# Moving the bias of three heads to GpSimd, holding exp(bias) in PSUM, and one store per batch, in a log-sum-exp kernel

## The chip, the cores and the metric

The kernel runs on one core of one Trainium2 chip. The metric is the device time of one execution in microseconds (us). The core has five engines, named in the profile as PE (TensorE), DVE (VectorE), ACT (ScalarE), POOL (GpSimd) and SP (SyncE, which issues the loads here). Sixteen DMA engines move data between HBM and SBUF.

## The reference

```python
def reference(x, bias):            # x [8, 2048, 2048] f32, bias [8, 256] f32
    B, S, D = x.shape
    H = bias.shape[0]
    Dh = D // H                    # 256
    x_heads = x.reshape(B, S, H, Dh).transpose(0, 2, 1, 3)
    x_heads = x_heads + bias[None, :, None, :]
    x_tiled = np.repeat(x_heads, 2, axis=2)
    mx = x_tiled.max(axis=-1, keepdims=True)
    lse = mx.squeeze(-1) + np.log(np.exp(x_tiled - mx).sum(axis=-1))
    return lse                     # [8, 8, 4096]
```

So for each row and each of eight heads the kernel needs log(sum(exp(x + bias))) over 256 elements, and stores each result twice. It reads 134 MB and writes 1 MB. The kernels leave out the maximum, which these inputs allow.

## The kernel before

The input is cut into 64 tiles of 256 rows (2 MB). In a tile each of 128 partitions holds K = 2 rows. Nine tile buffers take the loads, all issued by SP. The eight heads of a row go two ways:

- Heads 0 and 1 ("biased"): TensorE adds the bias by matmul into PSUM, ScalarE takes exp there and sums by its accumulator.
- Heads 2 to 7 ("weighed"): ScalarE takes exp(x) in place, and VectorE multiplies by exp(bias), which is held in SBUF, and sums, one instruction per head and row.

```python
    def weigh(v, h, dst):                       # L180: one head of one row
        nc.vector.tensor_tensor_reduce(out=j, in0=v, in1=w_rep[:, c : c + Dh],
            scale=1.0, scalar=0.0, op0=ALU.mult, op1=ALU.add, accum_out=dst)
    ...
    for t in range(T):
        for k0, k1, c0, c1 in pieces(t):        # one piece, except in the last two tiles
            ...
            if c0 == 0:
                got = add_bias([xt[:, k, 0:CPE] for k in range(k0, k1)])   # TensorE, L155, L160
            w0 = max(c0, CPE)
            if w0 < c1:
                exp_inplace(xt[:, k0:k1, w0:c1])                           # ScalarE, L174
            if c0 == 0:
                for k in range(k0, k1):
                    sum_biased(got[k - k0], lambda h: sum_at(k, h))        # ScalarE, L166
            for k in range(k0, k1):
                for c in range(w0, c1, Dh):
                    weigh(xt[:, k, c : c + Dh], c // Dh, sum_at(k, c // Dh))
        ...
        if t + NBUF < T:
            load(t + NBUF)
        ...                                     # every 8 tiles: transpose, Ln, store of a batch
```

A batch of 8 tiles ends in a 64-row result, 2 KB per row, which leaves in five stores of uneven row counts, such as `[16, 16, 16, 9, 7]` (the table `STORE_ROWS`).

The softmax here doesn't subtract the row's maximum and nothing guards it: scores larger than these inputs give would overflow.

## Time and profile before

| | before |
|---|---|
| time, median of 3 runs | 342.96 us (342.44 to 343.75) |
| span in the profile | 341.4 us |
| loads | about 429 GB/s while they run, 2 MB per 4.9 us |
| VectorE, one tile | 12 multiply-and-sums, 0.347 us start to start: 4.16 us |
| ScalarE, one tile | 4.44 us |
| matmuls of tile 61 start, having waited for its load | 321.5 us |
| from there to the end | 19.9 us |

First the page of the profile: the span, the busy line (busy us, share, number of instructions), the DMA share and the GB/s in 40 slices of the span, and two of the DMA queues (packets, MB, share of 16 engines' time). q1 carries the loads and stores; q14 fetches instructions.

```profile
span 341.4 us, 3425 instructions
...
PE 235.2 (69%) x410; PEld 69.7 (20%) x410; DVE 271.6 (80%) x1538; ACT 295.2 (86%) x597; POOL 10.4 (3%) x22
...
DMA  8999999999999999999999999999999999999910
GB/s 302 430 430 429 427 430 427 426 425 426 424 429 429 430 429 419 431 426 429 430 424 425 428 428 427 379 402 428 430 419 389 397 428 429 396 380 397 366 57 16
...
q1 hardware_dynamic: 11168, 135.17, 94.8%
...
q14 instruction: 20, 0.16, 0.1%
```

The DMA engines are busy from the first slice to the 38th. No compute engine is. So the stream of loads bounds the kernel, except for the last 20 us. The rate dips after slice 25. The loads share SP's queue with stores, which SP issues from 64 us on, so the stores alone do not say why the dips begin so late.

The groups of instructions (line, engine, operation, shapes, count, then busy us and mean ns of one, then idle time before them and what ended it):

```profile
L180 DVE CUSTOM_DVE_ANT_0 junk<-xt,w_rep 128x256 f32<-128x256 f32 x768 | 270.8, 422 | 65.7 <-ACT xt L174 65.6
...
L174 ACT ACTIVATE xt<-xt 128x3072 f32<-128x3072 f32 x62 | 171.2, 2762 | 24.5 <-DMA xt<-in_x_dram 19.9 <-DVE R L180 4.0
```

VectorE waits for ScalarE, and ScalarE waits for data. Both have time to spare per tile.

Stretches of 5 us (start and end; then busy us and number of instructions of PE, PEld, DVE, ACT, POOL; granted clock; DMA share; GB/s):

```profile
200.00:205.00 5.00, 4.15 (x10) 0.91 (x8) 4.24 (x24) 4.60 (x10) 0.00 (x0) 0.88 1.01 429
220.00:225.00 5.00, 4.60 (x12) 1.44 (x11) 4.35 (x26) 4.82 (x11) 0.00 (x0) 0.83 0.95 372
300.00:305.00 5.00, 4.43 (x8) 1.52 (x8) 4.36 (x27) 4.81 (x10) 0.00 (x0) 0.66 0.98 356
320.00:325.00 5.00, 4.10 (x6) 1.17 (x4) 4.27 (x25) 4.52 (x10) 0.00 (x0) 0.50 0.74 282
325.00:330.00 5.00, 5.00 (x10) 1.46 (x10) 5.00 (x31) 4.73 (x12) 0.00 (x0) 0.75 0.24 71
```

VectorE issues 24 to 27 counted instructions in 5 us, because each multiply-and-sum is followed by an instruction that reads the accumulator out. At 325 us the loads are over and VectorE is full.

Last, the timeline at tile 61 (start, duration, engine, instruction, and in brackets the idle time and what ended it), and the last Ln on ScalarE:

```profile
321.54 3.78 PE L160 MATMUL ps<-xt,ident 128*128 128x512 f32 x4 [0.90 <-DMA xt<-in_x_dram]
...
338.64 0.37 ACT L209 ACTIVATE res<-tps 8x256 f32<-8x256 f32 x1 [0.94 <-PE tps L196]
```

TensorE waits for tile 61 until 321.54 us.

### The profile page before, as it was taken

What the parts mean: (1) busy time and instruction counts of PE and PEld (TensorE: products, weight loads), DVE (VectorE), ACT (ScalarE), POOL (GpSimd) and SP (SyncE); (2) the same over time, 40 slices, a digit from 0 to 9 for tenths busy, and PEclk for the clock granted to TensorE, in tenths of its full rate; (3) what the DMA queues carried; (4) which work ended last, traced back from release to release, by engine and by line L of the source; (5) the groups of instructions that cost most, each with busy time, mean ns of one, the idle gap of its engine ahead of it and who ended that gap; (6) DMA issues with size and microseconds to landing.
All of it is one profiled execution on the core that took longest, in us unless ns stands there. A gap on an engine that the chain in (4) does not pass through costs nothing. (4 is left out here: it accounts for less than half of the span.)

```text
span 341.4 us, 3425 instructions
## 1 busy us (share of the span) xinstructions
PE 235.2 (69%) x410; PEld 69.7 (20%) x410; DVE 271.6 (80%) x1538; ACT 295.2 (86%) x597; POOL 10.4 (3%) x22
## 2 busy tenths in 40 slices
PE   6295788767786767775767775965775665775791
PEld 2121122112121112221121221321221221221220
DVE  0429999898887888887889688787798698797795
ACT  2389999998997998987997997998998998998895
POOL 6000000000000000000000000000000000000004
PEclk9999856885868885888885886588888888888585
DMA  8999999999999999999999999999999999999910
GB/s 302 430 430 429 427 430 427 426 425 426 424 429 429 430 429 419 431 426 429 430 424 425 428 428 427 379 402 428 430 419 389 397 428 429 396 380 397 366 57 16
DMA packets 11545, 135.50 MB, mean 397 GB/s; under 512 B 1913, under 2 KB 2185, under 8 KB 3329
## 3 DMA queue, kind: packets, MB, share of 16 engines
q1 hardware_dynamic: 11168, 135.17, 94.8%
q0 software_dynamic: 352, 0.10, 0.1%
q14 instruction: 20, 0.16, 0.1%
q8 instruction: 3, 0.05, 0.1%
q10 hardware_dynamic: 2, 0.01, 0.0%
HBM read 134.23 MB, written 1.05 MB: 396 GB/s over the span
## 5 line engine op out<-in xcount | busy, mean ns | idle before, releaser
L180 DVE CUSTOM_DVE_ANT_0 junk<-xt,w_rep 128x256 f32<-128x256 f32 x768 | 270.8, 422 | 65.7 <-ACT xt L174 65.6
L160 PE MATMUL ps<-xt,ident 128*128 128x512 f32 x256 | 184.3, 859 | 88.6 <-DMA xt<-in_x_dram 88.3
L174 ACT ACTIVATE xt<-xt 128x3072 f32<-128x3072 f32 (+3 forms) x70 | 177.7, 2541 | 24.5 <-DMA xt<-in_x_dram 19.9
L166 ACT ACTIVATE ps<-ps 128x256 f32<-128x256 f32 x256 | 94.6, 369 | 11.7 <-PE ps L160 6.7
L160 PEld LDWEIGHTS ps<-xt,ident 128*128 128x128 f32 x256 | 57.4, 248 | 173.2 <-DMA xt<-in_x_dram 124.2
L180 DVE DVE_READ_ACCUMULATOR2_ANT R<- 128x1 f32 x744 | 61.9, 83 | 0.0
L155 PE MATMUL ps<-b,ones 3*128 3x512 bf16 x128 | 46.6, 447 | 6.2 <-DVE R L180 6.2
L166 ACT ACTIVATION_READ_ACCUMULATOR ps<-ps 128x1 f32 x256 | 48.6, 190 | 0.0
L155 PEld LDWEIGHTS <-ones 3*128 3x128 bf16 x128 | 7.5, 97 | 74.5 <-issue 66.7
L230 POOL DMA_DIRECT2D out_dram<-res x8 | 4.0, 505 | 324.1 <-ACT res L209 324.1
L136 PE MATMUL ps<-brow,ones 1*128 1x512 f32 x6 | 5.5, 1074 | 3.2 <-DMA brow<-in_bias_dram 3.2
L209 ACT ACTIVATE res<-tps 64x512 f32<-64x512 f32 (+3 forms) x11 | 5.9, 540 | 1.4 <-PE tps L196 0.9
L143 ACT ACTIVATE w_rep<-ps 128x512 f32<-128x512 f32 x3 | 1.8, 597 | 5.5 <-PE ps L136 5.5
L196 PEld LDWEIGHTS tps<-ident,R 128*64 128x64 f32 (+1 forms) x16 | 2.7, 166 | 8.9 <-issue 4.7
L196 PE MATMUL tps<-ident,R 128*64 128x128 f32 (+1 forms) x16 | 4.3, 363 | 0.0
L196 PE MATMUL tps<-ident,Rz 128*8 128x128 f32 x2 | 0.7, 374 | 4.7 <-DVE Rz L180 4.7
L136 PEld LDWEIGHTS ps<-brow,ones 1*128 1x128 f32 x6 | 1.8, 321 | 5.3 <-issue 5.3
L110 ACT ACT_TABLE_LOAD x1 | 1.3, 1283 | 0.7 <-PEq L307 0.7
L132 POOL DMA_DIRECT2D b<-bparts x3 | 1.6, 553 | 0.0
L196 PEld LDWEIGHTS tps<-ident,Rz 128*8 128x8 f32 x2 | 0.2, 82 | 5.2 <-DVE Rz L180 2.6
L129 POOL TENSOR_TENSOR brest<-brest,bparts 1x512 f32<-1x512 f32 x1 | 1.1, 1146 | 0.1
L127 POOL TENSOR_TENSOR brest<-brow,bparts 1x512 f32<-1x512 f32 x1 | 1.1, 1144 | 0.1
(15 smaller groups left out, 5.7 us busy)
## 6 DMA issues: line engine op xcount, KB each, us to landing
xt<-in_x_dram SPq DMA_DIRECT2D x62, 2048.0 KB
xt<-in_x_dram SPq DMA_DIRECT2D x2, 1024.0 KB
xt<-in_x_dram SPq DMA_DIRECT2D x2, 512.0 KB
xt<-in_x_dram SPq DMA_DIRECT2D x3, 256.0 KB
out_dram<-res SPq DMA_DIRECT2D x17, 32.0 KB
xt<-in_x_dram SPq DMA_DIRECT2D x2, 128.0 KB
out_dram<-res POOLq DMA_DIRECT2D x8, 12.0 KB, 1.7
out_dram<-res SPq DMA_DIRECT2D x3, 24.0 KB
```

Of the source, the lines that this page charges most:

```text
L110: nc.scalar.add_instruction(mybir.InstLoadActFuncSet(name=nc.get_next_instruction_name(), act_func_set_id=set_idx,))
L132: nc.gpsimd.dma_start(out=b3[i : i + 1, :], in_=bparts[:, i])
L136: nc.tensor.matmul(ps[i], lhsT=ones, rhs=brow[:, CPE + c : CPE + c + MM], start=True, stop=True,)
L143: nc.scalar.activation(out=w_rep[:, c : c + MM], in_=ps[i], func=ACT.Exp)
L155: nc.tensor.matmul(p[:, 0:CPE], lhsT=ones3, rhs=b3, start=True, stop=False)
L160: nc.tensor.matmul(p[:, 0:CPE], lhsT=ident, rhs=v, start=False, stop=True)
L166: nc.scalar.activation(out=p[:, c : c + Dh], in_=p[:, c : c + Dh], func=ACT.Exp, accum_out=dst(h),)
L174: nc.scalar.activation(out=v, in_=v, func=ACT.Exp)
L180: nc.vector.tensor_tensor_reduce(out=j, in0=v, in1=w_rep[:, c : c + Dh], scale=1.0, scalar=0.0, op0=ALU.mult, op1=ALU.add, accum_out=dst,)
L196: nc.tensor.transpose(out=tps[i][0:nr, k], in_=src(k), identity=ident)
L209: nc.scalar.activation(out=rv, in_=tv, func=ACT.Ln)
L230: engine.dma_start(out=ov, in_=iv)
```

## The change

The intent is to relieve VectorE. In 62 of 64 tiles, three of the six weighed heads take another way: GpSimd adds their bias in SBUF ahead of exp (`g_add`), ScalarE takes exp one tile later, and VectorE sums all three heads of both rows with one instruction (`g_sum`). exp(bias) of the other heads lies in PSUM, so that VectorE's multiply reads only one operand from SBUF, while GpSimd works there. To make room, the PSUM buffers of the biased heads go from six to four, and the two of the transposes share one tile. A buffer is given back one tile later. And each batch leaves in one store of 64 rows, in place of five. The last two tiles stay on the old way.

```diff
 NPE = 2
+NG = 3
+NLATE = 2
 NBUF = 9
-STORE_ROWS = [
-    [15, 14, 13, 12, 10],
-    ...
-]
@@
-    w_rep = sb.tile([P, CW], F32, name="w_rep")
+    b_rep = sb.tile([P, NG * Dh], F32, name="b_rep")
@@
-    ps = [pp.tile([P, MM], F32, name=f"ps{i}") for i in range(6)]
+    w_rep = pp.tile([P, CW], F32, name="w_rep")
+    ps = [pp.tile([P, MM], F32, name=f"ps{i}") for i in range(4)]
... (the two transpose tiles become one; b_rep and w_rep are filled)
@@
+    def g_add(t):
+        nc.gpsimd.tensor_tensor(out=g_part(t), in0=g_part(t), in1=b_tile, op=ALU.add)
+
+    def g_sum(t):
+        b, blk = divmod(t, NBLK)
+        nc.vector.tensor_reduce(
+            out=R[b][:, :, NPE : NPE + NG, blk],
+            in_=g_part(t).rearrange("p k (h j) -> p k h j", j=Dh),
+            op=ALU.add,
+            axis=mybir.AxisListType.X,
+        )
@@
-            step, parts = n, STORE_ROWS[b]
+            step, parts = n, [nr]
@@
-        for k0, k1, c0, c1 in pieces(t):
+        if left >= NLATE:
+            got = add_bias([xt[:, k, 0:CPE] for k in range(K)])
+            g_add(t)
+            w0 = CPE + NG * Dh
+            exp_inplace(xt[:, :, w0:D])
+            if t:
+                exp_inplace(g_part(t - 1))
+            for k in range(K):
+                sum_biased(got[k], lambda h: sum_at(k, h))
+            for k in range(K):
+                for c in range(w0, D, Dh):
+                    weigh(xt[:, k, c : c + Dh], c // Dh, sum_at(k, c // Dh))
+            if t:
+                g_sum(t - 1)
+        for k0, k1, c0, c1 in pieces(t) if left < NLATE else []:
@@
-        if t + NBUF < T:
-            load(t + NBUF)
+        if left == NLATE:
+            exp_inplace(g_part(t))
+            g_sum(t)
+        if 0 < t and t - 1 + NBUF < T:
+            load(t - 1 + NBUF)
```

More of the change, by code (lines that the diff above doesn't have):

```diff
@@ L19 @@
 NPE = 2
+NG = 3
+NLATE = 2
 NBUF = 9
 LAST_CUTS = [[0, 1024, 2048], [0, 512, 1024, 1536, 1792, 2048]]
-STORE_ROWS = [
-    [15, 14, 13, 12, 10],
-    [11, 9, 16, 16, 12],
-    [16, 16, 16, 8, 8],
-    [16, 16, 16, 9, 7],
-    [16, 16, 16, 10, 6],
-    [16, 16, 16, 11, 5],
-    [16, 16, 16, 12, 4],
-]
 @with_exitstack
@@ L76 @@
     xts = [sb.tile([P, K, D], F32, name=f"xt{i}") for i in range(NBUF)]
-    ps = [pp.tile([P, MM], F32, name=f"ps{i}") for i in range(6)]
-    tps = [pp.tile([P, K, P], F32, name=f"tps{i}") for i in range(2)]
+    w_rep = pp.tile([P, CW], F32, name="w_rep")
+    ps = [pp.tile([P, MM], F32, name=f"ps{i}") for i in range(4)]
+    tpair = pp.tile([P, 2, K, P], F32, name="tpair")
+    tps = [tpair[:, i] for i in range(2)]
     def pieces(t):
@@ L132 @@
         nc.gpsimd.dma_start(out=b3[i : i + 1, :], in_=bparts[:, i])
-    for i, c in enumerate(range(0, CW, MM)):
+    for c in range(0, CW, MM):
         nc.tensor.matmul(
-            ps[i],
+            w_rep[:, c : c + MM],
             lhsT=ones,
@@ L142 @@
         )
-        nc.scalar.activation(out=w_rep[:, c : c + MM], in_=ps[i], func=ACT.Exp)
+    nc.scalar.activation(out=b_rep, in_=w_rep[:, 0 : NG * Dh], func=ACT.Copy)
+    for c in range(0, CW, MM):
+        w = w_rep[:, c : c + MM]
+        nc.scalar.activation(out=w, in_=w, func=ACT.Exp)
     n_ps = [0]
@@ L171, in sum_biased, with g_part @@
             )
+    b_tile = bass.AP(
+        tensor=b_rep.tensor,
+        offset=b_rep.offset,
+        ap=[b_rep.ap[0], [0, K], [1, NG * Dh]],
+    )
+    def g_part(t):
+        return xts[t % NBUF][:, :, CPE : CPE + NG * Dh]
+    def g_add(t):
[7 more added lines that the diff above has]
+            axis=mybir.AxisListType.X,
+        )
     def exp_inplace(v):
```

## The prediction

> **What bounds the kernel now.** The load stream. In the table of 5 us stretches the DMA share is about 1.0 from 5 to 320 us, at 420 to 433 GB/s for the first 210 us: a 2 MB tile every 4.9 us. In the timeline of a steady tile ScalarE needs 4.44 us (one 128x3072 exp, 2.65 us start to start, then four 128x256 exps with accumulator reads, 1.79 us) and VectorE 12 multiply-and-sums at 347 ns, 4.16 us. Both wait for data (groups: VectorE idle 65.7 us before the multiply-and-sum). The trace's landing times show one of 16 DMA engines drifting some 7 us behind the rest by the end; the instruction fetches in the span, 15 of 8 KB (0.32 us each) and three of 16 KB (1.06 us), would about explain it if all are on it (my inference). The tile-61 matmuls wait for data until 321.5 us. The tail after it, 17 us to the last Ln plus 2.7 us for the store, is compute: the chain of waits names ScalarE, and VectorE runs without a gap from 324.4 to 333.4 us.
>
> **What changes, per tile (62 of 64).**
> - GpSimd: one 128x1536 add. A 1x512 fp32 add took 1.146 us; scaled, 3.4 us, under 4.9. The multiply now has one input in PSUM, the sum has only one, so VectorE should not hold GpSimd off[...]. No run here shows it yet.
> - VectorE: six multiply-and-sums go, one 128x1536 sum comes[...], 1.7 us. 6x0.347+1.7 = 3.8 us.[...]
> - ScalarE: one 3072 exp becomes two of 1536 (1.37 us each in the tail): 4.53 us per tile. Still under 4.9; it catches up more slowly after the late start.
> - Buffers return one tile later; depth was 7 to 8 tiles, so no starvation.
> - Stores: one of 64 rows per batch instead of five uneven ones. It takes one place in the queue, so the dips to 360 to 400 GB/s after 210 us should shrink, but those are idle fast engines; the slowest decides.[...] fewer instruction fetches: -0.6 us.
>
> **Critical path.** Nothing saved on VectorE is on it in the stream. In the tail ScalarE has one more 1536 exp after tile 61 lands (tile 60's delayed group), +1.4 us; VectorE two sums for six multiplies, +1.3 us, overlapped. So 343 + 0.3 + 1.5 = 344.8 us.
>
> **Prediction: 344.8 us, 8 in 10 between 342.3 and 349. Faster by over 2%: 3%; within 2%: 86%; slower: 11%.**
>
> **Right or wrong by:** GpSimd adds at 3.2 to 3.6 us; sums at 1.7 us; multiply-and-sums every 0.35 to 0.41 us; ScalarE busy up about 5 us; tile 61 landing at 321 to 323 us; tail 21 to 22 us; DMA share still 1.0 until 320.
>
> **What would make it wrong:** GpSimd over 4.9 us per tile, or blocked by VectorE; PSUM reads much slower (VectorE near 4.9 us); the even stores delaying the slow DMA engine by several us; or the dips costing real time, so that the single store brings tile 61 up to 5 us earlier.

The sum: 343 + 0.3 + 1.5 = 344.8 us. The 0.3 in it is made of -0.6 us for the fetches and of +0.9 us for rows that the slow DMA engine would write more with even stores; without that term the sum would be 343.9 us. That VectorE should not hold GpSimd off was an assumption at this point; the run a_w_sbuf tests it.

## The result, and the profile after

| | before | after |
|---|---|---|
| time, median | 342.94 us (4 runs) | 337.94 us (4 runs, 337.88 to 338.08) |
| ratio | | 0.9853, 95% interval 0.9833 to 0.9872 |
| span in the profile | 341.4 us | 336.1 us |
| tile 61's matmuls start | 321.5 us | 315.2 us |
| from there to the end | 19.9 us | 20.9 us |

A ratio here is the mean time of one kernel's runs over that of the other's runs of the same rounds, so it is not quite the ratio of the medians quoted. All later ratios are against the kernel before in the same rounds.

The kernel is 1.5% faster. The predicted range (342.3 to 349 us) missed; that the change stays within 2%, to which the prediction gave 86%, came true. The page after:

```profile
span 336.1 us, 2806 instructions
...
PE 235.5 (70%) x410; PEld 69.4 (21%) x410; DVE 244.6 (73%) x856; ACT 300.6 (89%) x660; POOL 224.2 (67%) x84
...
DMA  8999999999999999999999999999999999999910
GB/s 297 427 431 435 421 429 425 437 423 426 425 432 425 435 422 431 427 430 424 430 426 425 431 427 430 422 429 433 429 426 429 424 427 431 423 435 416 365 43 16
...
q1 hardware_dynamic: 10832, 135.17, 95.1%
...
q14 instruction: 15, 0.12, 0.1%
```

The dips in GB/s are gone. VectorE has 856 counted instructions in place of 1538, and q14 fetched 15 blocks in place of 20. The groups:

```profile
L182 POOL TENSOR_TENSOR xt<-xt,b_rep 128x1536 f32<-128x1536 f32 x62 | 213.8, 3449 | 95.6 <-DMA xt<-in_x_dram 89.6
...
L200 DVE CUSTOM_DVE_ANT_0 junk<-xt,w_rep 128x256 f32<-128x256 f32 x396 | 140.4, 417 | 86.5 <-ACT xt L194 86.5
...
L186 DVE TENSOR_REDUCE R<-xt 128x6 f32<-128x1536 f32 x62 | 108.4, 1749 | 0.7 <-ACT xt L194 0.7
```

GpSimd's add takes 3.449 us (predicted 3.4), the sum 1.749 us (1.7), and the multiply with one operand in PSUM 0.417 us, no longer than the 0.422 us from SBUF. The same five stretches after:

```profile
200.00:205.00 5.00, 2.62 (x7) 0.86 (x6) 3.80 (x13) 4.69 (x11) 3.56 (x2) 0.94 1.00 426
220.00:225.00 5.00, 2.62 (x7) 0.79 (x6) 3.79 (x14) 4.72 (x11) 3.56 (x2) 0.99 0.99 423
300.00:305.00 5.00, 4.26 (x8) 1.14 (x7) 3.80 (x13) 4.68 (x11) 3.55 (x2) 0.66 1.00 426
320.00:325.00 5.00, 4.85 (x9) 1.54 (x10) 4.27 (x15) 4.97 (x8) 0.00 (x0) 0.66 0.19 57
325.00:330.00 5.00, 1.22 (x4) 0.10 (x3) 4.17 (x25) 4.91 (x17) 2.06 (x5) 1.00 0.03 7
```

In the steady stretches nothing bounds the kernel but DMA, as before, and at the same rate. But between 320 and 325 us there is almost nothing left to load, where before had 282 GB/s. The timeline:

```profile
315.18 1.98 PE L159 MATMUL ps<-xt,ident 128*128 128x512 f32 x4 [0.76 <-DMA xt<-in_x_dram]
...
333.15 0.37 ACT L229 ACTIVATE res<-tpair 8x256 f32<-8x256 f32 x1 [0.93 <-PE tpair L216]
```

So the whole gain, and more, is that tile 61 lands 6.4 us earlier. The tail is 1.1 us longer, as predicted in kind (1.5 us).

### Where the 6.4 us could come from

The trace also records when each of the 16 DMA engines finished its part of a load. In both kernels the last landing falls further and further behind the others, and the tile is there only when it has come: tile 61 has its last landing at 321.50 us in before and at 315.14 us in after, and its matmuls start at 321.54 and 315.18 us. The records do not name the engine; that it is the same one each time is read from the lag, which grows in steps. The following is worked out from those landings (lag of the last engine behind the median of the 16) and from the packet records (q14 blocks of 8 KB; the number of VectorE instructions in the trace up to that time, waits on semaphores included). Listed are the blocks that are followed at once by a 16 KB data packet of 1.26 to 1.27 us, where the usual one takes 0.612 us, and those at the same step of VectorE's count where another block hides that packet (212.8 us after). The list of before stops where the dips begin.

```
before: block fetched at us     31.7  54.1  76.5  101.1  127.2  153.6  182.5  207.9
        VectorE instructions      79   205   329    452    579    705    849    970
        lag of last engine, us   1.1   2.1   3.1    4.1    5.1    6.1    7.1    8.1

after:  block fetched at us     37.7  79.0  122.5  167.8  212.8  258.6  308.2
        VectorE instructions      69   196    325    451    577    703    843
        lag of last engine, us   0.9   1.8    2.9    3.8    4.5    5.4    6.2
```

The pattern is clear. About every 126 VectorE instructions a block is fetched (8192 bytes over 126 are 65 bytes an instruction, an estimate), and with each the last engine falls back by about 1 us: 0.32 us for the block and 1.27 - 0.61 = 0.66 us by which the next data packet is late. Before, VectorE runs some 25 instructions per tile, so a block every 5 tiles, 12 before tile 61. After, 14 per tile, 7 blocks before tile 61. Five blocks at 0.98 us are 4.9 us.

That is one theory, the **fetch theory**: the gain comes from VectorE's smaller number of instructions, through the DMA engine that fetches them. Its rival is the **store theory**, which my prediction had named as what could make it wrong: five stores hold places in SP's queue (their issues take 19.8 to 20.8 us of SP's timeline in each of the first six batches of before, 0.5 us for the one store of after), the loads behind them are issued late, and the dips in GB/s are the cost. The two make opposite claims about undoing one part alone. A third view, that VectorE's or GpSimd's busy time as such matters, is tested on the way.

### The profile page after: what moved, and what is told of

Its sections match the earlier page's. It is cut to its first block, busy times and chain, and to the rows that moved or that the text cites. A ratio compares the mean times of both kernels' runs of the same rounds, so it can differ in the third digit from the quotient of the medians.

```text
span 336.1 us, 2806 instructions
## 1 busy us (share of the span) xinstructions
PE 235.5 (70%) x410; PEld 69.4 (21%) x410; DVE 244.6 (73%) x856; ACT 300.6 (89%) x660; POOL 224.2 (67%) x84
## 4 chain that ended last, share of the span: by engine, by line
DMA 71%; DVE 6%; ACT 5%; PE 1%; issue 1%; SPq 0%; ACTq 0%; DVEq 0%
DMA xt<-in_x_dram 71%; ACT xt L194 4%; DVE junk L200 3%; DVE R L186 2%; ACT ps L165 1%; PE ps L159 1%; ACT res L229 0%; PE tpair L216 0%; DVE Rz L200 0%; DVE R L200 0%; SPq L95 0%; ACTq L194 0%; DVEq L356 0%
## 5 line engine op out<-in xcount | busy, mean ns | idle before, releaser
L182 POOL TENSOR_TENSOR xt<-xt,b_rep 128x1536 f32<-128x1536 f32 x62 | 213.8, 3449 | 95.6 <-DMA xt<-in_x_dram 89.6
L200 DVE CUSTOM_DVE_ANT_0 junk<-xt,w_rep 128x256 f32<-128x256 f32 x396 | 140.4, 417 | 86.5 <-ACT xt L194 86.5
L194 ACT ACTIVATE xt<-xt 128x1536 f32<-128x1536 f32 (+1 forms) x132 | 183.4, 1435 | 13.5 <-DMA xt<-in_x_dram 12.5
L186 DVE TENSOR_REDUCE R<-xt 128x6 f32<-128x1536 f32 x62 | 108.4, 1749 | 0.7 <-ACT xt L194 0.7
L165 ACT ACTIVATE ps<-ps 128x256 f32<-128x256 f32 x256 | 94.6, 369 | 10.5 <-PE ps L159 6.3
L154 PE MATMUL ps<-b,ones 3*128 3x512 bf16 x128 | 48.7, 454 | 14.5 <-ACT ps L165 7.9
L200 DVE DVE_READ_ACCUMULATOR2_ANT R<- 128x1 f32 x372 | 30.6, 82 | 0.0
L132 PE MATMUL w_rep<-brow,ones 1*128 1x512 f32 x6 | 5.5, 1078 | 3.5 <-DMA brow<-in_bias_dram 3.5
L229 ACT ACTIVATE res<-tpair 64x512 f32<-64x512 f32 (+3 forms) x11 | 5.9, 539 | 1.2 <-PE tpair L216 0.9
L216 PE MATMUL tpair<-ident,R 128*64 128x128 f32 (+1 forms) x16 | 3.6, 310 | 2.0 <-DVE R L186 2.0
L216 PEld LDWEIGHTS tpair<-ident,R 128*64 128x64 f32 (+1 forms) x16 | 2.0, 130 | 9.1 <-DVE R L186 3.9
```

The costliest lines, as they stand in the source:

```text
L132: nc.tensor.matmul(w_rep[:, c : c + MM], lhsT=ones, rhs=brow[:, CPE + c : CPE + c + MM], start=True, stop=True,)
L154: nc.tensor.matmul(p[:, 0:CPE], lhsT=ones3, rhs=b3, start=True, stop=False)
L165: nc.scalar.activation(out=p[:, c : c + Dh], in_=p[:, c : c + Dh], func=ACT.Exp, accum_out=dst(h),)
L182: nc.gpsimd.tensor_tensor(out=g_part(t), in0=g_part(t), in1=b_tile, op=ALU.add)
L186: nc.vector.tensor_reduce(out=R[b][:, :, NPE : NPE + NG, blk], in_=g_part(t).rearrange("p k (h j) -> p k h j", j=Dh), op=ALU.add, axis=myb ...
L194: nc.scalar.activation(out=v, in_=v, func=ACT.Exp)
```

## The experiments

Times are medians of four runs (three rounds and the profiled run). "Tile 61" is the start of its matmuls in the profile, which wait for the load. "VectorE instr." is the count on the page, without waits. Ratios are against before in the same rounds. Differences of some 0.4 us of one trace to another are not resolved.

| kernel | VectorE instr. | q14 blocks | tile 61, us | time, us | ratio (95%) |
|---|---|---|---|---|---|
| before | 1538 | 20 | 321.5 | 342.94 | |
| b_one_store | 1538 | 20 | 320.2 | 341.71 | 0.9966 (0.9947 to 0.9985) |
| after | 856 | 15 | 315.2 | 337.94 | 0.9853 (0.9833 to 0.9872) |
| a_five_stores | 856 | 15 | 315.6 | 338.30 | 0.9865 (0.9850 to 0.9879) |
| a_pad_dve | 1600 | 21 | 320.3 | 343.12 | 1.0006 (0.9991 to 1.0021) |
| a_pad_pool | 856 | 21 | 315.6 | 338.13 | 0.9861 (0.9846 to 0.9876) |
| a_no_gpsimd | 856 | 14 | 315.1 | 338.00 | 0.9853 (0.9836 to 0.9871) |
| a_w_sbuf | 856 | 15 | (428.7) | 452.24 | 1.3149 (1.3076 to 1.3222) |
| a_skip_load | 856 | 15 | 324.0 | 346.98 | 1.0115 (1.0094 to 1.0137) |
| a_row0 | 856 | 15 | 314.8 | 337.65 | 0.9857 (0.9835 to 0.9879) |
| a_nlate5 | 889 | 16 | 315.0 | 336.68 | 0.9815 (0.9798 to 0.9831) |
| a_ng4 | 608 | 13 | 313.5 | 336.68 | 0.9823 (0.9807 to 0.9838) |
| few | 236 | 10 | 311.7 | 335.42 | 0.9788 (0.9770 to 0.9806) |
| few_nlate5 | 299 | 11 | 312.2 | 333.86 | 0.9742 (0.9726 to 0.9758) |

In a_w_sbuf tile 61 waits for compute, not for its load.

### b_one_store: the single store alone

```diff
 # the kernel before
-            step, parts = n, STORE_ROWS[b]
+            step, parts = n, [nr]
```

> The kernel before, with one thing of the change alone: one 64-row store per batch in place of five uneven ones. Store theory (the five stores take places in the load queue, and so delay the loads; the single store is what brought tile 61 in 6.4 us earlier): about 336.5 us, with tile 61 landing near 315 us. Fetch theory (each 8 KB refill of VectorE's instructions holds one DMA engine up for 0.98 us, and VectorE still runs 25 instructions per tile here): the dips in GB/s after 210 us disappear, the slow engine's lag behind the bulk is then 11 to 12 us at the end instead of 8 (the bulk is no longer held back), tile 61 still lands at 321 to 322.5 us, time 342.5 to 344 us.

Measured: 341.71 us, tile 61 at 320.2 us. The page's rate and instruction queue, and the timeline at tile 61:

```profile
GB/s 296 430 430 427 429 430 425 426 426 425 432 425 427 428 428 429 425 428 427 430 430 420 428 430 427 435 421 426 430 430 430 423 422 427 439 428 407 200 50 17
...
q14 instruction: 20, 0.16, 0.1%
```

```profile
320.23 3.75 PE L160 MATMUL ps<-xt,ident 128*128 128x512 f32 x4 [0.17 <-DMA xt<-in_x_dram]
```

The dips are gone, and still only 1.3 of the 6.4 us came. The last engine's lag at tile 60, measured against the time by which the bytes of 61 tiles have arrived in all, is 10.7 us here and 7.1 us in before. So the five stores cause the dips, but the dips were mostly time that the faster engines would have gained in vain. The store theory falls as the main cause. The 1.3 us is more than the fetch theory foresaw (its range allowed tile 61 no earlier than 321), and the time fell below its 342.5 us. The single store is worth a little.

### a_five_stores: the change without the single store

```diff
 # the kernel after
-            step, parts = n, [nr]
+            step, parts = n, STORE_ROWS[b]
```

> The changed kernel with the five uneven stores per batch put back, nothing else. Store theory: about 344 us. Fetch theory: 337 to 338.5 us[...].

Measured: 338.30 us, tile 61 at 315.6 us. The fetch theory's range holds, and the store theory's 344 us is excluded.

```profile
315.62 3.30 PE L170 MATMUL ps<-xt,ident 128*128 128x512 f32 x4 [2.43 <-DMA xt<-in_x_dram]
```

### a_pad_dve and a_pad_pool: idle instructions

744 memsets of one column, which nobody reads, on VectorE or on GpSimd.

```diff
 # the kernel after, in the branch left >= NLATE
+            for i in range(12):
+                nc.vector.memset(pad[:, i : i + 1], 0.0)      # a_pad_dve
+                nc.gpsimd.memset(pad[:, i : i + 1], 0.0)      # a_pad_pool, in its place
```

> The changed kernel with 12 memsets of 128x1 more per tile on VectorE (62 tiles, 744 instructions), into a scratch column that nobody reads. VectorE has the time for it: 3.8 us of 4.9 per tile, and some 0.7 us more. Fetch theory: 744/126 = 5.9 refills more, at 0.98 us each: +5.8 us, 343 to 344.5 us, and the slow engine's lag behind the bulk at the end 11 to 12 us in place of 6.2. Store theory, or any theory in which VectorE's work and not its instruction count matters: 337.9 to 338.5 us.

> The changed kernel with the same 744 memsets on GpSimd instead. The refills are as many as with VectorE's, but I expect them on another DMA engine, because in the trace of after the refills that coincide with ScalarE's and PE's counts of instructions do not move the slowest landing. Fetch theory with one DMA engine for each instruction stream: within 0.6 us of 337.9. If all streams shared the slow engine: 343 to 344.5 us. Store theory: 337.9 us.

Measured: 343.12 us with the memsets on VectorE, 338.13 us with them on GpSimd. Both fetched 21 blocks in place of 15. From the pages of the two, and their timelines (tile 61), VectorE's kernel first:

```profile
q14 instruction: 21, 0.17, 0.1%
...
320.28 1.99 PE L160 MATMUL ps<-xt,ident 128*128 128x512 f32 x4 [2.42 <-DMA xt<-in_x_dram]
```

```profile
q14 instruction: 21, 0.17, 0.1%
...
315.63 1.99 PE L160 MATMUL ps<-xt,ident 128*128 128x512 f32 x4 [0.79 <-DMA xt<-in_x_dram]
```

This is the strongest pair. The memsets, 59 ns each, raised VectorE's busy time by 9.3 us over the whole span (253.9 from 244.6 us), well within its idle time, and put tile 61 back by 5.1 us, which is the whole difference between b_one_store and after. The same number of instructions and of fetched blocks on GpSimd moved it by 0.4 us, no more than traces differ. So it is not the number of blocks that counts, but whose they are. The lag of the last engine at tile 60, measured as above, is 10.5 us in a_pad_dve (6.1 in after, 5.9 in a_pad_pool). The reading that fits is that GpSimd's blocks go to another DMA engine, which has time; no view names the engine of a block. Nor do VectorE's memsets delay the stream by giving buffers back later: the bytes of 61 tiles had arrived by 304.8 us in a_pad_dve and by 304.2 us in after, so the bulk was 0.6 us later, while the last engine finished tile 60 5.1 us later. The forecast for a_pad_dve, 343 to 344.5 us, holds. Its size, 5.8 us, was over the 5.1 us measured because only five of the six further blocks came before tile 61 (12 blocks, the last at 299.7 us, in place of 7; the next came at 325.0 us). Five at 0.98 us are 4.9 us.

### a_no_gpsimd: the change without GpSimd's work

Wrong results: without `g_add` three heads miss their bias.

```diff
 # the kernel after
-            g_add(t)
```

> Wrong results on purpose: the changed kernel without GpSimd's adds. It asks what GpSimd's part costs or is worth by itself in time. Fetch theory: nothing, 337.4 to 338.1 us, the same number of VectorE instructions and the same landing of tile 61 within 0.5 us. If GpSimd's reads and writes in SBUF slowed the loads or the other engines: faster than 337 us.

Measured: 338.00 us, tile 61 at 315.1 us. The work that gives the change its name, 214 us of GpSimd, costs nothing and by itself gains nothing. What it buys is that VectorE can sum six head-rows with one instruction in place of twelve (six multiply-and-sums, each with its accumulator read).

### a_w_sbuf: exp(bias) in SBUF

```diff
 # the kernel after
-    w_rep = pp.tile([P, CW], F32, name="w_rep")
+    w_ps = pp.tile([P, CW], F32, name="w_ps")
+    w_rep = sb.tile([P, CW], F32, name="w_rep")
...
-        w = w_rep[:, c : c + MM]
-        nc.scalar.activation(out=w, in_=w, func=ACT.Exp)
+        nc.scalar.activation(
+            out=w_rep[:, c : c + MM], in_=w_ps[:, c : c + MM], func=ACT.Exp
+        )
```

> The changed kernel with exp(bias) copied to SBUF as in the kernel before, so each multiply-and-sum has two SBUF inputs while GpSimd adds. If the two engines lock each other out for whole instructions[...], the 3.45 us add and the six multiplies of 2.1 us can't overlap: 5.5 us per tile instead of 4.9, 375 to 390 us, with GpSimd adds or multiplies that last longer in the profile. If they do not contend: 337.9 us.

Measured: 452.24 us. The timeline shows the lock at work: a multiply that starts while GpSimd adds lasts as long as the add, and goes on just after.

```profile
199.39 3.67 POOL L184 TENSOR_TENSOR xt<-xt,b_rep 128x1536 f32<-128x1536 f32 x1 [3.30 <-DMA xt<-in_x_dram]
...
199.69 3.65 DVE L202 CUSTOM_DVE_ANT_0 junk<-xt,w_rep 128x256 f32<-128x256 f32 x1
...
203.27 0.41 DVE L202 CUSTOM_DVE_ANT_0 junk<-xt,w_rep 128x256 f32<-128x256 f32 x1
```

The page's busy line shows what bounds it now:

```profile
PE 240.2 (53%) x410; PEld 70.5 (16%) x410; DVE 429.1 (95%) x856; ACT 297.0 (66%) x660; POOL 230.1 (51%) x84
```

The mechanism was as expected and the size was not: I had 375 to 390 us. In the trace 56 multiplies, for 62 adds, lasted over 3 us, and the multiplies together took 329 us in place of 140. Between 100 and 400 us VectorE is never idle, and GpSimd makes 44 adds: 6.8 us per tile. That is about one stalled multiply of 3.6 us, five of 0.35 us and the sum of 1.7 us, 7.0 us in all (an estimate from the timeline). My forecast of 5.5 us per tile had left VectorE's sum out. With one operand in PSUM, in after, no multiply took over 0.423 us. So the PSUM part of the change is what makes the GpSimd part free.

### a_skip_load and a_row0: which DMA engine

a_skip_load splits one tile's load into 120 and 8 partitions, so that an engine is left out of most of it. a_row0 splits each batch's store into 60 rows and four stores of one row. In the landings the two parts of the load used 15 and 8 engines, and a one-row store used one.

```diff
 # a_skip_load: the kernel after, in load(t), for tile 24
+            for p0, p1 in [(0, 120), (120, P)]:
                 nc.sync.dma_start(
-                    out=xts[t % NBUF][:, k0:k1, c0:c1], in_=rows_of(t)[:, k0:k1, c0:c1]
+                    out=xts[t % NBUF][p0:p1, k0:k1, c0:c1],
+                    in_=rows_of(t)[p0:p1, k0:k1, c0:c1],
                 )
 # a_row0: the kernel after
-            step, parts = n, [nr]
+            step, parts = n, [nr - 4, 1, 1, 1, 1]
```

> The changed kernel, but the load of one tile (24) is split into 120 partitions and 8 partitions. [...] Fetch theory, if the slow engine is that last one: its lag of 6 us falls under the second slowest engine's 3 us, so tile 61 lands about 3.2 us earlier, 334.5 to 335.5 us.[...] If the load stream as a whole and not one engine's share bounded the time: 337.9 or a little more.

> The changed kernel with each batch's 64-row store split into 60 rows[...] and four stores of one row[...]. If VectorE's refills land on that lowest engine, it gets 4 rows of 0.084 us more in each of 7 batches: tile 61 lands about 2.4 us later, 340 to 341 us, and the landings of the one-row stores come as late as the slowest landing of the loads around them. If the slow engine is another[...]: tile 61 within 0.5 us of after, 337.5 to 338.5 us, and the one-row stores land early.

"That last one" stands for an engine that the split was to leave out, "that lowest engine" for the one that the one-row stores use.

a_skip_load missed every forecast: 346.98 us. The split load itself was slow; the page shows it in slices 15 and 16:

```profile
GB/s 303 428 428 435 426 426 429 428 430 427 428 425 431 428 219 229 429 428 426 429 426 430 426 426 425 434 429 428 426 429 432 429 425 421 433 430 418 349 52 15
```

The landings had 15 engines on the first part and 8 on the second, but the rate halved for two slices of 8.6 us: between 122 and 138 us 104 of the 217 data packets took over 1.2 us, where the usual one takes 0.612 us. Why was not tried. For the question it was meant for it still gives a hint. The engine that the first part left out had at least 7 packets of 0.612 us less of this tile, 4.3 us (an estimate: a load is 128 packets of 16 KB, 8 for each of 16 engines, and the second part has one for each of its 8). After that load the last engine's lag was 3.0 us (at 140 us), as in after (2.9 us), and not less, which speaks against the slow engine being the one that the split relieved.

a_row0 took 337.65 us, and the one-row stores landed early: at 211.3 us, 1.1 us after the median of the neighbouring 60-row store, whose last engine was 4.2 us behind. So the slow engine is not the one that they used. In a_five_stores the stores of 5 rows, on five engines, do include a landing as late as the loads' last one (at 295.5 us, 4.5 us behind the store's median at 291 us). The slow engine is then one of the five that a store of 5 rows used, and by the one-row stores not the one that those used. That is an inference from landings; no view names the engine.

The landings of before also show what the stores cost this engine. Each of the 30 stores of the six batches that leave before tile 61, down to the one of 5 rows, has as many landings as rows, and one of them far behind the store's median: 3.1 us in the first batch, 8.1 to 9.1 us in the sixth. So the slow engine seems to have a row of each, 30 rows, where it has 24 of the single stores if 64 rows are spread evenly over the 16 engines. At 0.084 us a row the single store should help by 0.5 us (an estimate), and not cost the 0.9 us of the prediction's cut term. Measured at tile 61: 1.3 us in before's setting, 0.4 us in after's, which is no more than traces differ. The rest of the 1.3 us is open.

### a_nlate5: the tail

```diff
 # the kernel after
-NLATE = 2
+NLATE = 5
```

> The changed kernel with the last five tiles on the old way in place of two (NLATE 5). The predicted tail cost, one more 1536 exp on ScalarE after tile 61 lands (1.4 us), is then taken back: the tail from tile 61's landing to the end 19.9 us as before in place of 20.9. VectorE has 30 instructions more, a quarter of a refill. Time 336.9 to 337.5 us. If the tail is not bound by ScalarE, 337.9.

Measured: 336.68 us, a little better than foreseen. Tile 61 at 315.0 us, the end at 334.9: a tail of 19.9 us, as before. So the added tail came from the delayed group of tile 60, and it can be avoided by going back to the old way a few tiles earlier. That its exp on ScalarE costs the time, and not its sum, is read from the trace of after: ScalarE is busy 9.68 of the 10 us from 315 us on, and the chain that ended last runs over it from 319.7 to 330.5 us.

### a_ng4, few and few_nlate5: fewer VectorE instructions still

If instructions on VectorE cost time through their fetch, then more of them can go. a_ng4 gives GpSimd four heads. few also replaces the remaining multiply-and-sums by one multiply and one sum per tile. few_nlate5 adds the cure of the tail.

```diff
 # a_ng4, few, few_nlate5: the kernel after
-NG = 3
+NG = 4
 # few, few_nlate5
-            for k in range(K):
-                for c in range(w0, D, Dh):
-                    weigh(xt[:, k, c : c + Dh], c // Dh, sum_at(k, c // Dh))
+            w_mul(t)       # tensor_tensor, 128x1024, times exp(bias) from PSUM, in place
             if t:
                 g_sum(t - 1)
+            w_sum(t)       # tensor_reduce, 128x1024 to 128x4
 # few_nlate5
-NLATE = 2
+NLATE = 5
```

> The changed kernel with four heads on GpSimd in place of three (NG 4), nothing else. VectorE goes from 14 to about 10 instructions per tile, so about two refills fewer before tile 61 (5 in place of 7), 1.0 us each. GpSimd's add becomes 4.6 us per tile (3.449 us times 4/3), still under 4.9. Fetch theory: tile 61 lands at 313 to 313.5 us, time 335.5 to 336.5 us. If GpSimd can't keep up: slower than 338 us.

> As a_ng4, and the two heads left to VectorE's multiply are done by one multiply (128x1024, exp(bias) from PSUM) and one sum per tile: about 4 VectorE instructions per tile in place of 14, VectorE's time per tile about 4.5 us. Fetch theory: two refills before tile 61 in place of seven, so VectorE's DMA engine is no longer last; the second slowest engine's lag of 3 us now decides. Tile 61 lands about 3 us earlier, at 311.5 to 312.5 us, time 334 to 335.5 us. If VectorE's busy time were what counts: 338 us or slower, since VectorE is busier than in a_ng4.

> As few, with the last five tiles on the old way (NLATE 5, which gave 1.3 us in a_nlate5). About 60 VectorE instructions more than few, half a refill. 333 to 334.5 us: the fastest of all if both gains add.

Measured: 336.68, 335.42 and 333.86 us. Tile 61 comes at 313.5 and 311.7 us in the first two, as forecast, and at 312.2 us in the third. a_ng4's time missed its range by 0.2 us. few is the case against busy time: its VectorE is busier than after's (290.9 us, or 4.5 us a tile, for 244.6 us), with a quarter of the instructions, and it is faster. Its busy line, queue and timeline:

```profile
PE 233.4 (70%) x410; PEld 69.0 (21%) x410; DVE 290.9 (87%) x236; ACT 300.7 (90%) x660; POOL 291.7 (88%) x84
...
q14 instruction: 10, 0.08, 0.1%
...
311.69 3.78 PE L159 MATMUL ps<-xt,ident 128*128 128x512 f32 x4 [0.97 <-DMA xt<-in_x_dram]
```

In few the last engine's lag is 2.8 us near the end, which is about what the second slowest had in after (3.0 us). From there VectorE's instructions no longer decide. few_nlate5 beats both kernels: 0.9742 of before, some 1.2% under after by the medians (333.86 and 337.94 us, of different rounds).

## Why the prediction was right or wrong

- **"What bounds the kernel now. The load stream"**, up to tile 61, with a compute tail: right. Both kernels end about 20 us after tile 61.
- **GpSimd's add, VectorE's sum, ScalarE's cost**: right. 3.449, 1.749 us and 5.4 us more of busy ScalarE (300.6 from 295.2), for 3.4, 1.7 and about 5.
- **"VectorE should not hold GpSimd off"**: right, and shown by its opposite: with exp(bias) in SBUF a multiply stalled for 3.65 us and the kernel took 452 us. The multiply with one operand in PSUM took no longer: 0.417 us against 0.422.
- **"Nothing saved on VectorE is on it in the stream"**: right for time, wrong for instructions. VectorE's busy microseconds are indeed off the critical path. Its instruction count is on it.
- **"the dips ... are idle fast engines; the slowest decides"**: right in the main. b_one_store removed the dips and gained 1.3 us at tile 61, where the dips look like 5.6 us (429 GB/s less the rate, summed over the stretches from 205 to 320 us, and divided by 429).
- **The tail, +1.5 us**: right in kind, 1.1 us measured.
- **The step that failed is the term for the landing of tile 61**: "fewer instruction fetches: -0.6 us", and the +0.9 us for the even stores, together +0.3 us. It measured -6.4 us. The mechanism of the fetches was in the text, even with the guess that all fetches explain the drifting engine, and its size was wrong twice. I took two blocks fewer; five fewer (7 in place of 12) fell on that engine before tile 61, since every multiply-and-sum counts double with its accumulator read. (The prediction's 15 blocks of 8 KB in before was a miscount as well: the page has 20.) And I took 0.32 us for each, the time of the block's own packet; each cost 0.98 us, because the data packet after it comes 0.66 us late. That gives 4.9 us, and the experiments, with five blocks between the two kernels each time, show 5.05 (b_one_store to after) and 5.10 (after to a_pad_dve). The term that is cut had the wrong sign: by inference from the landings the slow engine has a row of each of before's stores, and the single store gave 1.3 us instead of costing 0.9.
- **The sum, corrected**: before's span 341.4, less 1.3 for the stores, less 5.05 for the fetches, plus 1.1 for the tail, is 336.1 us. This only splits the measured difference into its parts, each read from these same traces, and so must come out. The check that could have failed is the fetch term: 4.9 us, worked out from the blocks, against 5.05 and 5.10 measured.

What stays open: why a data packet behind a block of VectorE's is 0.66 us late; which of the 16 DMA engines it is; what the single store saves beyond the rows; and why a load split into 120 and 8 partitions ran at half the rate.

## What to carry to other kernels

When a kernel is bound by its loads, look at the slowest of the 16 DMA engines, not at the mean rate. Here a tile was there when the last engine had landed (tile 61 of before at 321.50 us, its matmuls at 321.54 us), and a small extra load on that one engine was paid in full (five more blocks of 8 KB before tile 61 in a_pad_dve: 5.1 us). By the fetch theory, which the runs bear out, instruction fetch was such a load, so on an unrolled kernel at the DMA bound like this one, fewer and larger instructions on one engine (here VectorE) can be worth time even when that engine has time to spare (few: 236 counted instructions and 335.42 us, after: 856 and 337.94 us). Test it with a pad of idle instructions on that engine, and the same pad on another: the pair separates instruction count from work in one go (343.12 us with the pad on VectorE, 338.13 us on GpSimd).
